# The channel transform of a pair's first token tile, taken relative to the second tile's, in a Fourier mixing layer

## The chip, the cores and the metric

The kernel runs on one core of one Trainium2 chip. The metric is the device time of one execution in microseconds (us), smaller is better. Three runs of the kernel before took 1577.05, 1577.85 and 1578.53 us; the median is 1577.85 us. The core has a matrix engine (PE, whose weight loads are shown apart as PEld), a vector engine (DVE), a scalar engine (ACT), a general engine (POOL) and a queue engine (SP) that issues most loads. Each engine works through its own instructions in the order in which they stand; semaphores make it wait for others.

## The reference

Two sequences, x_prompt of 2048 tokens and x_sample of 512 tokens with 1024 channels each, go through two layers and a final norm. The first layer is windowed attention and is not touched here. The second mixes positions and channels by a Fourier transform and multiplies the result by a gate:

```python
def fourier_layer(x, g, w_gate, w_out):
    b, s, d = x.shape
    h = rmsnorm(x, g)
    hg = h.astype(jnp.float32).reshape(b, s, N_FGROUPS, FGROUP_CH)
    f = jnp.fft.fftn(hg, axes=(1, 3), norm="ortho").real
    f = f.reshape(b, s, d).astype(x.dtype)
    gate = h @ w_gate
    return x + (f * jax.nn.silu(gate)) @ w_out
```

All arithmetic is float32. On PE a float32 operand is cut into a rounded high part and a low rest ("hi" and "lo"), and a product is the sum of two or three matmuls over these parts.

## The kernel before

**Pairs.** The Fourier layer goes over the tokens in 20 tiles of 128 tokens. A Pair is two tiles; there are ten pairs, numbered 0 to 9. Pairs 0 and 1 hold the four tiles of the sample; pairs 2 and 3, 4 and 5, 6 and 7, 8 and 9 hold four tiles each of the prompt, tiles a, a+4, a+8 and a+12. For each pair two things are made from its normed input: the gate product (128 tokens by 1024 channels times 1024 by 1024, for both tiles), and the channel transform z of each tile (each group's 256 channels by a 256x256 matrix of cosines and sines, named chan or ch).

**The gate product in seven products.** The tile's channels are turned so that they lie on partitions. A11 and A12 are the two halves of the first tile's channels, A21 and A22 those of the second's; half 0 of a group is its first 128 channels, half 1 the other 128. The two-by-two block product is computed in the Winograd form with seven products, whose left factors are A11, A12, A22 and four sums, made by Pair.sums (lines 1106 to 1119) and cut into hi and lo by Pair.parts (line 1121):

- F[1] = A21 + A22
- F[2] = F[1] - A11
- F[3] = A11 - A21
- F[4] = A12 - F[2], which is (A11 + A12) - (A21 + A22)

S[i] are the hi and lo of F[i]. F[1] and F[2] share one tile named s1, F[3] and F[4] another named s4; both take a slot of a pool with four slots (tag "x", xtile), which the input tiles and the tile c of gate sums use as well. Line 1103 makes A21 - A22, whose hi and lo are named diff (tile tTd).

**The channel transform.** For the second tile (i = 1), z_odd_even (line 1143) uses that the even outputs of a 256-point transform need only the sum of the two halves, and the odd outputs only their difference: it multiplies S[1] and diff, each by a 128-column half of the matrix. The matrix's hi and lo stand side by side as 256 moving columns, so that one product takes two matmuls (hi and lo of the token side); 16 matmuls of 128x256 fill four PSUM banks. ACT copies the part of the matrix's lo out of a bank (line 1160), DVE adds the part of the hi (line 1161). For the first tile (i = 0), Pair.z (line 1124) multiplies A11 and A12 by the matrix directly, three matmuls for a product: 24 matmuls of 128x256 in two banks, through matmul3 (line 117), each emptied by one ACT instruction (line 1139).

**The four-point step.** When both pairs of a group are done, combine (line 1327) calls radix4 (line 1263): six DVE instructions of 128x1024 over the four z tiles, whose outputs POOL stores (line 1337), for the last group keeps.

**The loop and the queues.** gates(pr, hooks) (line 1184) writes out the seven products of one pair on PE: W = A11 B11, Z = S[1] T1, W += S[2] T2, Z += S[4] B22, W += S[3] T3, W += A22 N4, and X = A12 B21 in four steps (x_step) between them. Between the products stand hooks, in which the next pair nx is made ready: hook 1 and 2 turn its tiles (PE transposes, "trb", line 1089) and make F[1], diff, F[2], F[4] and their parts; hook 3 the parts of F[4], hook 4 F[3] and its parts; hook 5 is z_odd_even, hook 6 is z for the first tile and combine. The input tiles x of the pair after that are loaded by SP into freed slots of the pool "x" and normed (line 1056 on ACT: sum of squares; line 110 DVE and line 111 POOL: inverse root; line 1081 DVE: scaling). DVE adds the gate sums (c12 at line 1227, c22 at 1232, c11 at 1236), ACT takes tanh (line 1197), DVE finishes the gate (line 1198), POOL stores it.

A scheduler sets the final order on each engine from this text and its own estimates, and gives out the pool slots; PSUM for turns and z is a pool of five banks, for W, Z and X another of three. What an operand has to wait for is therefore set by three things: the data, the slot or bank, and what stands ahead in the queue.

In the rows below, "odd pair" and "even pair" name the number of nx, the pair being made ready; combine runs after the odd ones.

Of the kernel before, what the change touches and what calls it, by code (L numbers as in the profile page):

```python
# [14 lines left out]
ALU = mybir.AluOpType  # L15
# [27 lines left out]
def encoder(  # L43
# [61 lines left out]
    def htile(shape, dtype, name):  # L105
        return main.tile(shape, dtype, align_bytes=LINE, tag="hT", bufs=8, name=name)
# [884 lines left out]
    def fourier_phase(tail):  # L991
        with ExitStack() as es:
# [15 lines left out]
            def zt(name):  # L1008
                return right([P, D], F32, name)
# [58 lines left out]
            class Pair:  # L1068
# [71 lines left out]
                        out, ps.rearrange("p (g o n) -> p g o n", g=2, o=2), AF.Copy, scale=1.0 if t >= SEQ // P else 0.5  # L1140
                    )

                def z_odd_even(self):

                    t = self.ts[1]
                    self.zs[1] = zt(f"z{t}")
                    for g in range(4):
                        ps = bank(f"z{t}_{g}")
                        for odd, m in enumerate((self.S[1], self.diff)):

                            to = ps[:, odd * 256 : odd * 256 + 256].rearrange("p (a n) -> p a n", a=2)
                            for part in range(2):
                                PE.matmul(
                                    to, m[part][:, g * P : (g + 1) * P], ch[:, 0, :, odd * P : (odd + 1) * P],
                                    start=part == 0, stop=part == 1,
                                )
                        v = ps.rearrange("p (o a n) -> p a o n", o=2, a=2)
                        out = self.zs[1][:, g * 256 : g * 256 + 256].rearrange("p (n o) -> p o n", o=2)
                        scale = 1.0 if t >= SEQ // P else 0.5
                        ACT.activation(out, v[:, 1], AF.Copy, scale=scale)  # L1160
                        last_z[0] = DVE.scalar_tensor_tensor(out, v[:, 0], scale, out, ALU.mult, ALU.add)
# [98 lines left out]
            def tt(out, a, b, op):  # L1260
                DVE.tensor_tensor(out, a, b, op)

            def radix4(z, name):

                e = zt(f"e{name}")
                tt(e, z[0], z[2], ALU.add)
                tt(z[0], z[0], z[2], ALU.subtract)
                tt(z[2], z[1], z[3], ALU.add)
                tt(z[1], z[1], z[3], ALU.subtract)
                tt(z[3], e, z[2], ALU.subtract)  # L1270
                tt(e, e, z[2], ALU.add)
                return e, z[3], z[0], z[1]
# [50 lines left out]
            def turns4(pr):  # L1323
                pr.sums(3)
                pr.parts(3)

            def combine(pr):

                if pr.n % 2 == 0:
                    return  # L1330
                gi = pr.n // 2
                r = radix4(pairs[pr.n - 1].zs + pr.zs, f"r{gi}")
                if gi == 4:
                    kept.extend(r)
                    return
                for i in range(4):
                    POOL.dma_start(gsd[i] if gi == 0 else evd[gi - 1, i] if i < 2 else odd[gi - 1, i - 2], r[i])
# [20 lines left out]
            for n, pr in enumerate(pairs[:-1]):  # L1358
                nx = pairs[n + 1]
                if n:  # L1360
                    for i in range(2):
                        nx.load(1 - i)
                        nx.norms(1 - i)
                gates(pr, {
                    1: [lambda: turns1(nx)], 2: [lambda: turns2(nx)], 3: [lambda: turns3(nx)], 4: [lambda: turns4(nx)],
                    5: [lambda: nx.z_odd_even()],
                    6: [lambda: nx.z(0), lambda: nx.z(1), lambda: combine(nx)],
                })
            gfb = fp.tile([P, D], F32, tag="gb", bufs=1, name="gfb")
            SP.dma_start(gfb, bass.AP(gf.tensor, gf.offset, [[0, P], [1, D]]))  # L1370
# [616 lines left out]
```

## Time and profile before

| what | value |
|---|---|
| median of three runs | 1577.85 us |
| the profiled execution, its own time | 1577.83 us |
| span inside that execution | 1576.1 us |
| mean granted PE clock | 0.999 |
| the stage of the seven products, about | 1060 to 1320 us of the span |
| busy in that stage, 1060 to 1335 us (275 us) | PE 274.8, DVE 219.9, ACT 151.7, POOL 52.1 us |

The profile is one execution. Its page gives busy time by engine; the view of waits says which engine waited for which; the chain of waits follows the work that ended last, piece by piece; the timeline lists instructions with their start, duration, engine, line, operands and, in brackets, the idle time before them and what ended it. A matmul row shows the time in the pipeline; the time that a stretch of matmuls takes is read from the starts or from the chain. Consecutive instructions of DVE and ACT overlap a little, so the step from start to start is shorter than the duration.

### The profile page before, as it was taken

Reading aid. Unit: us, or ns where it says so; the run is one execution under the profiler, and the core shown is the slowest. Engines: PE = TensorE matmul, PEld = TensorE weight load, DVE = VectorE, ACT = ScalarE, POOL = GpSimd, SP = SyncE. Lnnn points to the kernel's source line nnn. Section 1 sums busy time; section 2 is a strip of 40 time slices with the busy share of each in tenths; the row PEclk is TensorE's granted clock in tenths of the full one; section 3 lists DMA queues with packets and bytes.
Section 4 is the critical chain, followed back from the end, with each engine's and each line's share of the span. In section 5 each row is a group of like instructions: output and inputs, shape, how many; then the busy total and the mean of one; then the engine's idle time right before and its main releaser. Section 6 shows DMA issues by size and latency. Waiting matters only on the chain.

```text
span 1576.1 us, 27737 instructions
## 1 busy us (share of the span) xinstructions
PE 1565.2 (99%) x9882; PEld 1315.6 (83%) x9882; DVE 1150.7 (73%) x2793; ACT 878.1 (56%) x2096; POOL 444.6 (28%) x614
## 2 busy tenths in 40 slices
PE   9999999999999999999999999999999999999998
PEld 7888888888888888988888888888888888888886
DVE  6888555877548786378764577668878778989886
ACT  7788535776247684257852477646655554333353
POOL 2575642421404314024223242222111111101100
PEclk9999999999999999999999999999999999999999
DMA  8598695565856667656649656675666569557852
GB/s 296 203 332 287 223 365 210 208 247 202 297 214 214 204 248 256 242 193 235 238 170 326 232 208 208 248 253 200 210 222 233 185 219 399 193 201 267 312 195 94
DMA packets 100997, 373.90 MB, mean 237 GB/s; under 512 B 11268, under 2 KB 22284, under 8 KB 83453
## 3 DMA queue, kind: packets, MB, share of 16 engines
q1 hardware_dynamic: 83148, 298.17, 53.7%
q0 software_dynamic: 16400, 70.04, 11.5%
q10 hardware_dynamic: 1312, 3.94, 0.6%
q8 instruction: 78, 1.28, 0.3%
q14 instruction: 59, 0.48, 0.1%
HBM read 280.84 MB, written 91.26 MB: 236 GB/s over the span
## 4 chain that ended last, share of the span: by engine, by line
PE 94%; DVE 4%; issue 1%; ACT 1%; DMA 0%; POOL 0%; SPq 0%; POOLq 0%; DVEq 0%; ACTq 0%
PE gp L117 14%; PE qp L117 14%; PE spt L117 11%; PE op L117 7%; PE W L117 7%; PE av L615 6%; PE spt L530 6%; PE fo L117 5%; PE vp L117 3%; PE Z L117 3%; PE pt L589 3%; PE Wo L117 3%; PE z L117 2%; PE X L117 2%; PE Zo L117 2%; PE ABp L117 1%
## 5 line engine op out<-in xcount | busy, mean ns | idle before, releaser
L117 PE MATMUL gp<-h,wg 128*128 128x512 f32 x960 | 237.7, 396 | 0.0
L117 PE MATMUL qp<-h,wq 128*128 128x512 f32 x960 | 237.0, 396 | 0.0
L549 DVE CUSTOM_DVE_ANT_0 S<-spt,b 128x385 f32<-128x385 f32 (+1 forms) x320 | 156.5, 528 | 105.5 <-PE spt L530 68.3
L117 PEld LDWEIGHTS gp<-h,wg 128*128 128x128 f32 x960 | 174.9, 188 | 37.3 <-issue 1.0
L117 PEld LDWEIGHTS qp<-h,wq 128*128 128x128 f32 x960 | 174.9, 188 | 36.4 <-issue 0.3
L557 ACT ACTIVATE S<-S 128x385 f32<-128x385 f32 (+1 forms) x320 | 188.8, 596 | 19.5 <-DVE S L549 19.3
L597 ACT CAST pts<-pt 128x384 fp32r<-128x384 f32 (+1 forms) x240 | 100.6, 458 | 167.0 <-PE pt L589 158.2
L598 DVE TENSOR_TENSOR pts<-pt,pts 128x384 fp32r<-128x384 f32 (+1 forms) x240 | 114.3, 520 | 23.4 <-ACT pts L597 22.2
L639 POOL TENSOR_TENSOR uT<-o,uT 128x256 fp32r<-128x256 f32 x75 | 55.6, 741 | 229.5 <-ACT uT L638 229.4
L117 PE MATMUL spt<-wo,uT 128*128 128x512 f32 x480 | 120.3, 391 | 0.0
L117 PE MATMUL op<-wo,uT 128*128 128x512 f32 x480 | 118.9, 391 | 0.0
L530 PE MATMUL spt<-kwin,qab 64*128 64x384 f32 (+1 forms) x960 | 118.8, 353 | 0.0
L615 PEld LDWEIGHTS av<-pts,v 128*128 128x128 f32 x576 | 101.4, 188 | 18.8
L615 PE MATMUL av<-pts,v 128*128 128x512 f32 (+1 forms) x576 | 115.7, 341 | 0.0
L117 PE MATMUL fo<-wo,tTu 128*128 128x512 f32 x480 | 115.4, 392 | 0.0
L117 PEld LDWEIGHTS op<-wo,uT 128*128 128x128 f32 x480 | 89.4, 188 | 18.5
L117 PEld LDWEIGHTS spt<-wo,uT 128*128 128x128 f32 x480 | 89.1, 188 | 18.3
L117 PEld LDWEIGHTS fo<-wo,tTu 128*128 128x128 f32 x480 | 88.3, 188 | 17.3
L569 DVE TENSOR_SCALAR S<-S 128x384 f32<-128x384 f32 (+1 forms) x192 | 95.9, 499 | 6.8
L530 PEld LDWEIGHTS spt<-kwin,qab 64*128 64x128 f32 x960 | 74.7, 186 | 28.4 <-issue 26.4
L635 POOL TENSOR_TENSOR o<-o,s 128x256 f32<-128x256 f32 x75 | 55.4, 738 | 134.5 <-DVE o L633 134.1
L589 PEld LDWEIGHTS pt<-ident,S 64*128 64x128 f32 x1328 | 78.3, 138 | 4.2 <-issue 2.1
(331 smaller groups left out, 3173.2 us busy)
## 6 DMA issues: line engine op xcount, KB each, us to landing
wo<-wsd SPq DMA_DIRECT2D x32, 1024.0 KB, 5.0
wq<-wsd SPq DMA_DIRECT2D x31, 1024.0 KB, 7.1
wg<-wsd SPq DMA_DIRECT2D x31, 1024.0 KB, 5.8
x<-x1d SPq DMA_DIRECT2D x40, 512.0 KB, 3.9
b<-b21d SPq DMA_DIRECT2D x40, 512.0 KB, 4.8
b<-rowd SPq DMA_DIRECT2D x40, 384.0 KB, 4.3
xs<-in_x_dram SPq DMA_DIRECT2D x23, 512.0 KB, 7.5
s2d<-gt POOLq DMA_DIRECT2D x40, 256.0 KB, 5.2
```

The source lines that it names most:

```text
L117: ins = pe(PE.matmul(out, a[i], b[j], start=start and i + j == 0, stop=stop and i == 1, skip_group_check=more))
L530: pe(PE.matmul(banks[j][:, 2 + k0 * P : 2 + k1 * P], res["q"][rows, qp, b * P : (b + 1) * P], kwin[g][rows, kp, b * P + k0 * P : b * P + k ...
L549: seq(DVE, DVE.tensor_tensor_reduce(out=s[:, e0:e1], in0=ps[:, 1 + e0 : 1 + e1], in1=st["bias"][:, j, 386 - e1 : 386 - e0][:, ::-1], scale ...
L557: last_exp[0] = seq(ACT, ACT.activation(s[:, e0:e1], s[:, e0:e1], AF.Exp, bias=s[:, 386:387], scale=-1.0, accum_out=s[:, 387:388]))
L569: seq(DVE, DVE.tensor_scalar(s[:, ks], s[:, ks], den, None, ALU.mult))
L589: pe(PE.transpose(ps[h][:, kb, j, :], ss[j][rows, 1 + kb * P : 1 + (kb + 1) * P], ident[rows, rows]))
L597: seq(ACT, ACT.copy(hi, ps[:, k0:k1]))
L598: seq(DVE, DVE.tensor_tensor(lo, ps[:, k0:k1], f32(hi), ALU.subtract))
L615: pe(PE.matmul(to, v, pt, start=n == part == 0, stop=part == 1 and n in (1, len(todo) - 1), skip_group_check=n > 1,))
L635: eng.tensor_tensor(o, o, s, ALU.mult)
L639: low = eng.tensor_tensor(lo, o, f32(hi), ALU.subtract)
```

## The change

For pairs 2 to 9 the first tile's transform is replaced by the transform of the first tile minus the second tile. The even outputs of that difference need F[4] (sum of halves of the difference), which is there as S[4]. The odd outputs need (A11 - A12) - (A21 - A22), which is 2 F[3] - F[4]: the new method cross makes it in place of F[4] with one DVE instruction, and cuts it into hi and lo in a new tile named tC (pool "hT", eight slots). z_odd_even is called a second time, with i = 0 and these two operands, in place of the two calls of z. The four-point step gets z0 - z1 and z2 - z3 in place of z0 and z2, and radix4_relative makes the same four outputs from them, in six DVE instructions again. Pairs 0 and 1 stay as they were.

```diff
+                def cross(self):
+
+                    F3, F4 = self.F[3], self.F[4]
+                    DVE.scalar_tensor_tensor(F4, F3, 2.0, F4, ALU.mult, ALU.subtract)
+                    self.mixed = split(htile([P, 2, 512], F32R, f"tC{self.n}"), F4)
+
-                def z_odd_even(self):
+                def z_odd_even(self, i=1):
 
-                    t = self.ts[1]
-                    self.zs[1] = zt(f"z{t}")
+                    t = self.ts[i]
+                    out_of = (self.S[1], self.diff) if i else (self.S[4], self.mixed)
+                    self.zs[i] = zt(f"z{t}")
                     for g in range(4):
                         ps = bank(f"z{t}_{g}")
-                        for odd, m in enumerate((self.S[1], self.diff)):
+                        for odd, m in enumerate(out_of):
...
+            def radix4_relative(z, name):
+
+                e = zt(f"e{name}")
+                tt(e, z[0], z[2], ALU.add)
+                tt(z[0], z[0], z[2], ALU.subtract)
+                tt(z[2], z[1], z[3], ALU.add)
+                tt(z[1], z[1], z[3], ALU.subtract)
+                DVE.scalar_tensor_tensor(z[2], z[2], 2.0, e, ALU.mult, ALU.add)
+                tt(z[0], z[0], z[1], ALU.add)
+                return z[2], e, z[0], z[1]
...
             def turns4(pr):
                 pr.sums(3)
                 pr.parts(3)
+                if pr.n > 1:
+                    pr.cross()
...
-                r = radix4(pairs[pr.n - 1].zs + pr.zs, f"r{gi}")
+                r = (radix4_relative if pr.n > 1 else radix4)(pairs[pr.n - 1].zs + pr.zs, f"r{gi}")
...
-                    6: [lambda: nx.z(0), lambda: nx.z(1), lambda: combine(nx)],
+                    6: [lambda: nx.z_odd_even(0) if nx.n > 1 else [nx.z(hf) for hf in range(2)], lambda: combine(nx)],
```

The lines of the changed kernel are shifted: the matmuls of z_odd_even are at line 1160 there (1153 before), its ACT and DVE instructions at 1167 and 1168 (1160 and 1161 before), tanh and gate at 1204 and 1205 (1197 and 1198), the gate sums c12, c22 and c11 at 1234, 1239 and 1243 (1227, 1232 and 1236); line 1146 is the new DVE instruction of cross. Numbers behind a name are buffer numbers of the program, not of the trace. Three places of the new order follow, all around pair 6, an even one.

PE at the end of gates for pair 5, where N4 (wN) ends and the first tile's transform stands. Names: chan_sb is the transform's matrix, tTb_0 and tTb_1 are A11 and A12 of pair 6, S_6_14299 is S[4], tC the new operand, wB the factor of the next pair's first product. Before:

```order
L117 MATMUL W_14167<-wN_3_12887,tTb_1_13953 128x512 x3
L117 MATMUL z_0_14369<-chan_sb,tTb_0_14241 128x256 x3
L117 MATMUL z_0_14369<-chan_sb,tTb_1_14253 128x256 x3
L117 MATMUL z_0_14369<-chan_sb,tTb_0_14241 128x256 x3
L117 MATMUL z_0_14369<-chan_sb,tTb_1_14253 128x256 x3
L117 MATMUL z_1_14383<-chan_sb,tTb_0_14241 128x256 x3
L117 MATMUL z_1_14383<-chan_sb,tTb_1_14253 128x256 x3
L117 MATMUL z_1_14383<-chan_sb,tTb_0_14241 128x256 x3
L117 MATMUL z_1_14383<-chan_sb,tTb_1_14253 128x256 x3
L117 MATMUL W_14415<-wB_0_12646,tTb_0_14241 128x512 x3
```

The same place now:

```order
L117 MATMUL W_14183<-wN_3_12887,tTb_1_13965 128x512 x3
L1160 MATMUL z_0_14389<-chan_sb,S_6_14299 128x256 x2
L1160 MATMUL z_0_14389<-chan_sb,tC_14330 128x256
L117 MATMUL W_14435<-wB_0_12646,tTb_0_14257 128x512 x3
L117 MATMUL W_14435<-wB_1_12664,tTb_0_14257 128x512
L1160 MATMUL z_0_14389<-chan_sb,tC_14330 128x256
L117 MATMUL W_14435<-wB_1_12664,tTb_0_14257 128x512
L1160 MATMUL z_1_14396<-chan_sb,S_6_14299 128x256 x2
L1160 MATMUL z_1_14396<-chan_sb,tC_14330 128x256 x2
L117 MATMUL W_14435<-wB_1_12664,tTb_0_14257 128x512
L117 MATMUL W_14435<-wB_2_12691,tTb_0_14257 128x512
L1160 MATMUL z_2_14403<-chan_sb,S_6_14299 128x256 x2
```

24 matmuls of 128x256 become 16 (each of z_0 to z_3 takes two with S[4] and two with tC), and in even pairs they are interleaved with the first matmuls of the next pair's W. The third matmul of the block needs the hi part of tC. In odd pairs the 16 stand together.

ACT in the same stretch. S_6 are casts of hi parts of the sums, jkb is the sum of squares of an input tile x, gt the tanh of gate sums, z the emptying of banks. Before:

```order
L1197 ACTIVATE gt_1_14279<-c_5_14234 128x512
L1013 CAST S_6_14310<-s_6_14256 128x512
L1056 ACTIVATE jkb_14400,ssb_14399<-x_14_14397 128x1024
L1197 ACTIVATE gt_1_14304<-c_14170 128x512
L1197 ACTIVATE gt_0_14319<-c_14170 128x512
L1160 ACTIVATE z_14323<-z_0_14324 128x2x128
```

Now:

```order
L1204 ACTIVATE gt_1_14295<-c_5_14250 128x512
L1167 ACTIVATE z_14343<-z_0_14344 128x2x128
L1167 ACTIVATE z_14343<-z_1_14351 128x2x128
L1204 ACTIVATE gt_1_14320<-c_14186 128x512
L1167 ACTIVATE z_14343<-z_2_14358 128x2x128
L1167 ACTIVATE z_14343<-z_3_14365 128x2x128
L1013 CAST S_6_14326<-s_6_14272 128x512
L1056 ACTIVATE jkb_14420,ssb_14419<-x_14_14417 128x1024
L1013 CAST tC_14330<-s_6_14272 128x512
L1204 ACTIVATE gt_0_14339<-c_14186 128x512
```

The cast of tC stands behind the sum of squares of x_14 (a tile that SP loads at that time), and four bank emptyings and a tanh stand ahead of both.

DVE in the same stretch, now, from the low part of S[2] to the first emptied bank (before, L1119, the sum F[3], came ahead of gt and c, and no L1146 and no tC were there):

```order
L1015 TENSOR_TENSOR S_6_14274<-s_6_14231,S_6_14274 128x512
L1234 TENSOR_TENSOR c_5_14250<-c_5_14250,Z_14184 128x512
L1015 TENSOR_TENSOR S_6_14299<-s_6_14272,S_6_14299 128x512
L1239 TENSOR_TENSOR c_14186<-c_14186,W_14183 128x512
L1205 SCALAR_TENSOR_TENSOR gt_1_14295<-gt_1_14295,c_5_14250 128x512
L1119 TENSOR_TENSOR s_6_14272<-trb_0_14252,s_6_14272 128x512
L1205 SCALAR_TENSOR_TENSOR gt_1_14320<-gt_1_14320,c_14186 128x512
L1146 SCALAR_TENSOR_TENSOR s_6_14272<-s_6_14272 128x512
L1015 TENSOR_TENSOR S_6_14326<-s_6_14272,S_6_14326 128x512
L1243 TENSOR_TENSOR c_14186<-c_14186,X_14185 128x512
L1015 TENSOR_TENSOR tC_14330<-s_6_14272,tC_14330 128x512
L1168 SCALAR_TENSOR_TENSOR z_14343<-z_0_14344,z_14343 128x2x128
```

The sum c22 (L1239) moved up by two rows, F[3] moved down behind it, and cross (L1146) stands behind F[3] and both gates; the low part of tC is the last reader of the tile s4, after which its slot can take the second input tile of the pair after.

On SP only the end of the stage differs: the load of one factor of X, b21_38, now stands behind two loads of wo in place of ahead of them.

More of the change, by code (lines that the diff above doesn't have):

```diff
@@ L1157, in z_odd_even @@
                         v = ps.rearrange("p (o a n) -> p a o n", o=2, a=2)
-                        out = self.zs[1][:, g * 256 : g * 256 + 256].rearrange("p (n o) -> p o n", o=2)
+                        out = self.zs[i][:, g * 256 : g * 256 + 256].rearrange("p (n o) -> p o n", o=2)
                         scale = 1.0 if t >= SEQ // P else 0.5
```

## The prediction

> **What bounds the kernel now.** First the busy time by engine on the page, which says PE; then, since such a share is a mean over stages, three views of the stage of the seven products.
>
> ```profile
> span 1576.1 us, 27737 instructions
> ...
> PE 1565.2 (99%) x9882; PEld 1315.6 (83%) x9882; DVE 1150.7 (73%) x2793; ACT 878.1 (56%) x2096; POOL 444.6 (28%) x614
> ```
>
> The view of waits for PE, then PEld, from 1050 to 1310 us (total, times, longest):
>
> ```profile
> PE trb L1089 <- DVE xrl L701: 0.3, 1, 0.3
> ...
> PEld z L1153 <- ACT S L1013: 0.3, 1, 0.3
> ```
>
> PE waits for nothing worth naming, so what leaves its queue leaves the time, if nothing else becomes late. The chain of waits over two pairs (start, us, work) gives the prices:
>
> ```profile
> 1136.48 1.91 PE z L1153 x16
> 1138.40 2.75 PE W L117 x12
> 1141.14 2.87 PE z L117 x24
> ...
> 1162.15 1.91 PE z L1153 x16
> 1164.06 2.75 PE W L117 x12
> 1166.81 2.87 PE z L117 x24
> ...
> 1175.83 0.87 PE trb L1089 x8
> ```
>
> The chain is PE without a gap; a pair lasts 1162.15 - 1136.48 = 25.67 us. The second tile's transform takes 1.91 us, the first tile's 2.87 us: both 0.1195 us a matmul. What stands beside it is the windows view (span, then busy us and instructions of PE, PEld, DVE, ACT, POOL, the granted clock): the first window holds an odd pair with the four-point step, the second an even pair.
>
> ```profile
> 1135.00:1160.00 25.00, 25.00 (x139) 21.67 (x138) 23.04 (x34) 13.86 (x27) 5.56 (x10) 1.00 0.72 246
> 1160.00:1185.00 25.00, 25.00 (x139) 21.67 (x138) 16.03 (x28) 13.50 (x28) 3.36 (x6) 1.00 0.47 168
> ```
>
> DVE is the engine to watch: nearly full in odd pairs, with room in even ones. The clock is granted in full.
>
> **The change part by part.**
>
> *PE.* Eight pairs (2 to 9) go from 24 matmuls to 16 of the same shape as the 16 that took 1.91 us: 8 x (2.87 - 1.91) = 7.7 us less. The Trainium skill, page "TensorE: Matmul & The Clock Gate", section "Back-to-back issue gap", gives an isolated gap of N/2.4 + 2.5 ns, 109 ns at 256 columns, by which this term would be 64 x 0.109 = 7.0 us and the sum below 1572.3 us. The chain's 0.1195 us differs, and the measurement decides.
>
> *DVE and ACT.* The prices of what is added (busy us, mean ns), from the groups by shape, 1000 to 1300 us:
>
> ```profile
> L1015 DVE TENSOR_TENSOR S<-s,S 128x512 fp32r<-128x512 f32 x40 | 27.5, 688 | 0.2
> L1081 DVE SCALAR_TENSOR_TENSOR x<-x,invb,g1b 128x1024 f32<-128x1024 f32 x20 | 25.6, 1280 | 13.2 <-POOL invb L111 13.2
> L1013 ACT CAST S<-s 128x512 fp32r<-128x512 f32 x40 | 24.9, 623 | 32.9 <-DVE s L1119 18.1 <-PE W L117 12.2 <-PE Z L117 2.5
> L1261 DVE TENSOR_TENSOR z<-z,z 128x1024 f32<-128x1024 f32 x13 | 15.9, 1225 | 0.4
> L1161 DVE SCALAR_TENSOR_TENSOR z<-z,z 128x256 f32<-128x256 f32 x40 | 14.4, 415 | 0.0
> L1139 ACT ACTIVATE z<-z 128x512 f32<-128x512 f32 x20 | 12.6, 632 | 8.3 <-PE z L117 8.2
> L1160 ACT ACTIVATE z<-z 128x256 f32<-128x256 f32 x40 | 12.6, 393 | 0.8 <-PE z L1153 0.8
> ...
> L1056 ACT ACTIVATION_READ_ACCUMULATOR jkb<-x 128x1 f32 x20 | 3.7, 186 | 0.0
> ```
>
> Per pair DVE gets cross (not in the trace; bounds 0.64, half of the 1.28 of L1081, and 0.69 of L1198 in the next rows, which has the same shape; I take 0.69), the low part of tC (0.69) and four emptied banks (4 x 0.415 = 1.66): 3.04 us. ACT gets one cast and four bank copies for two: 0.62 + 1.57 - 1.26 = 0.93 us. One of the six instructions of the four-point step becomes a scalar_tensor_tensor: between 1.225 and 1.28 us, at most 0.06 more four times, nothing. Over two pairs DVE's load goes from (23.04 + 16.03) x 25.67/25 = 40.1 us to 46.2 us, and the time for it from 51.3 to 49.4 us. It still fits, at 94%, so the cost is nothing as long as lateness in odd pairs is made up in even ones; with that cover gone it would be up to 3.04 us a pair. So the queue has to be walked through.
>
> *The odd pair.* The waits that DVE has to spare, timeline (start, duration, idle before in brackets):
>
> ```profile
> 1135.84 0.69 DVE L1232 TENSOR_TENSOR c<-c,W 128x512 f32<-128x512 f32 x1 [0.45 <-PE W L117]
> 1138.16 1.29 DVE L1198 SCALAR_TENSOR_TENSOR gt<-gt,c 128x512 f32<-128x512 f32 x2 [0.31 <-ACT gt L1197]
> 1139.37 1.41 DVE L1161 SCALAR_TENSOR_TENSOR z<-z,z 128x256 f32<-128x256 f32 x4
> 1140.70 1.27 DVE L1081 SCALAR_TENSOR_TENSOR x<-x,invb,g1b 128x1024 f32<-128x1024 f32 x1
> 1142.35 0.15 DVE L110 TENSOR_SCALAR invb<-ssb 128x1 f32<-128x1 f32 x1 [0.38 <-ACT jkb L1056]
> 1142.83 0.69 DVE L1198 SCALAR_TENSOR_TENSOR gt<-gt,W 128x512 f32<-128x512 f32 x1 [0.33 <-ACT gt L1197]
> 1152.16 0.68 DVE L1097 TENSOR_TENSOR tTb<-trb,tTb 128x512 fp32r<-128x512 f32 x1
> ```
>
> Back to back, instructions start closer together than they last: four emptied banks take 1140.70 - 1139.37 = 1.33 us, one of 512 columns 0.60 us (next rows). So DVE gets 1.33 + 2 x 0.60 = 2.53 us and has 0.45 + 0.31 + 0.38 + 0.33 = 1.47 us of waits to spend: at 1152.16, where the even pair begins, it is 1.1 us late if all the waits are filled, 2.5 if none. New waits for tanh and for the copies of the new banks come in their place; I take 2.0. PE arrives there 0.96 us earlier besides.
>
> *The even pair.* Its rows before:
>
> ```profile
> 1155.10 0.69 DVE L1097 TENSOR_TENSOR tTd<-trb,tTd 128x512 fp32r<-128x512 f32 x1 [0.28 <-ACT tTd L1096]
> ...
> 1158.10 0.68 DVE L1015 TENSOR_TENSOR S<-s,S 128x512 fp32r<-128x512 f32 x1
> ...
> 1158.86 0.32 SPq L1076 DMA_DIRECT2D x<-x1d  x1
> 1159.30 0.68 DVE L1015 TENSOR_TENSOR S<-s,S 128x512 fp32r<-128x512 f32 x1
> ...
> 1162.88 0.32 SPq L1076 DMA_DIRECT2D x<-x1d  x1
> ...
> 1166.93 1.06 ACT L1056 ACTIVATE jkb<-x 128x1024 bf16<-128x1024 f32 x1 [1.46 <-DMA x<-x1d]
> ...
> 1170.13 0.57 POOL L111 TENSOR_TENSOR invb<-invb,mhalf 128x1 f32<-128x1 f32 x1
> ...
> 1177.36 0.69 DVE L1097 TENSOR_TENSOR tTb<-trb,tTb 128x512 fp32r<-128x512 f32 x1 [5.34 <-ACT tTb L1096]
> ```
>
> With 2.0 - 0.28 = 1.7 us of lateness the low part of S[4] starts at 1161.0 instead of 1159.30. Then by the new order, at 0.60 a step: c22 at 1161.6, done 1162.3; gate, F[3], gate; cross at 1164.0, done 1164.7. N4 needs W's bank after c22: PE comes to it at 1164.06 - 0.96 = 1163.1, so that holds with 0.8 us to spare. PE wants the cast of tC after two matmuls of the new block, at 1166.81 - 0.96 + 0.24 = 1166.1. If ACT were free the cast would be done at 1164.7 + 0.6 = 1165.3, in time. But ahead of it stand four bank copies and a tanh (the banks fill from 1162.15 - 0.96 on, and c22 is done at 1162.3, which puts the last copy at about 1163.9), the cast of S[3] (to 1164.5), and the sum of squares of x (1.06 + 0.19 for its readout, to 1165.8): the cast ends at about 1166.4. PE waits 0.3 us, and 0.8 if DVE is 2.5 late; 0 if 1.1. I take 0.5 in pairs 4, 6 and 8. Pair 2 follows the old four-point step of pair 1, without the added work: nothing. Together 1.5 us, bounds 0 and 2.4. PE has other matmuls between its waits for the banks behind this one. The idle 5.34 us at 1177.36 is what the lateness falls into; the next odd pair starts clean.
>
> *The rest.* b21_38 on SP now stands behind two loads of wo:
>
> ```profile
> 1299.43 1.00 SPq L1713 DMA_DIRECT2D wo<-fbd  x2
> ...
> 1312.29 0.86 PE L117 MATMUL X<-b,tTb 128*128 128x512 f32 x3
> ...
> b<-b21d SPq DMA_DIRECT2D x20, 512.0 KB, 5.4
> ```
>
> Issued at about 1300.5 with 5.4 us to landing it is there at 1306, used at 1312: nothing.
>
> **Sum**, against the profiled execution's 1577.83 us (1.7 us of it lie around the span; the median shown is 1577.85, the same): 1577.83 - 7.7 + 1.5 = **1571.6 us**, that is -0.39%. About 0.2% (3.2 us) is what a measurement of this kernel tells from no change.
>
> **The rivals.**
>
> *No stall.* The cast of tC is in time everywhere: 1577.83 - 7.7 = 1570.1 us. For it: the bound of 1.1 us; against it: the sum of squares ahead of the cast, and that new waits tend to come where old ones are filled.
>
> *The load ahead of the cast is late.* The sum of squares needs an x tile whose load starts when the low part of S[2] is done: 1158.86 before, about 1160.6 now. How long the loads of x take, in 1130 to 1190 us:
>
> ```profile
> DMA to landing us min/median/max: 3.3/3.6/4.0
> ```
>
> At 3.3 to 3.6 us it lands by 1164.2, when ACT comes to it. At the 5.4 us of b21's loads, which have the same size, it lands at 1166.0 and the cast ends at 1167.9: PE waits 1.8 us, three times, 5.4 us in all, which leaves 1575.5 us. For it: lateness on DVE moves loads to where others run; against it: 4.0 was the longest of these loads.
>
> *The second x load makes the transposes late, and it is slower.* Its slot was that of s4, freed by the low part of S[3] (load at 1162.88); now it is freed by the low part of tC, about 1167.1 in even pairs. At 4.0 us it lands at 1171.1; sum of squares to 1172.4, inverse root to 1173.1 (0.15 on DVE, 0.57 on POOL), and since that small instruction stands ahead of both scalings on DVE, the first scaled tile is there at 1174.4; PE transposes it at 1175.83 - 0.96 + 0.5 = 1175.4. There is 1 us to spare, so up to a landing of 5 us nothing happens. From there each us is lost at the transposes and again where c22 and N4 follow late, about 2 us in each of four even pairs; the gain of 6.2 us is gone at 5.8 us. At 6 us: 1571.6 + 8 = 1579.6 us. For it: the slot is freed 4 us later than before, beside other traffic; against it: the same longest 4.0.
>
> *That the change doesn't do what it says* can be left out for the count: the order shows 16 for 24.
>
> **How the numbers follow.** Forecast (stall of 0.1 to 0.8 us in three pairs, 1570.4 to 1573) 0.52; no stall 0.17; late load or a like lateness at c22 or a bank (1573 to 1578) 0.23, a good third of it under 1574.7; slower 0.08. Faster by over 0.2% (under 1574.7): 0.52 + 0.17 + 0.08 = 0.77; within 0.2%: 0.15; slower: 0.08. The range leaves out half a us below the case without a stall, for the run's own spread, and the upper part of the late load: 1569.5 to 1576.5. The likeliest case alone has 1570.4 to 1573.
>
> **What would show it.** In the chain of waits the first tile's transform at 1.91 us in odd pairs, and pairs of about 24.7 us (odd) and 25.2 us (even); PE's instructions down by 64; in PE's or PEld's waits a new row, z at L1160 from ACT's cast (L1013), of about 0.3 to 0.8 us, three times; DVE near 46 us busy in two pairs; the second x load issued right after the low part of tC. Wrong would be: PE waiting for c22 (L1239), for trb from x (L1081), or for z banks from L1168, or a first-tile transform above 2 us without any wait.

## Result and profile after

| | before | changed | ratio (95% interval) |
|---|---|---|---|
| first series, median (runs) | 1578.19 us (14) | 1573.99 us (14) | 0.9974 (0.9966 to 0.9982) |
| second series, median (runs) | 1578.15 us (16) | 1575.42 us (11) | 0.9978 (0.9969 to 0.9987) |
| profiled execution | 1577.83 us | 1575.53 us | |
| its span | 1576.1 us | 1573.5 us | |

The change saves 4.2 us in the first series and 2.7 in the second; the forecast was 6.2. Both medians are faster by more than 0.2% and lie in the range given; the likeliest case alone (1570.4 to 1573) holds neither.

The busy times of the changed kernel, from the head of its page:

```profile
span 1573.5 us, 27706 instructions
...
PE 1561.3 (99%) x9818; PEld 1308.6 (83%) x9818; DVE 1169.3 (74%) x2841; ACT 884.9 (56%) x2120; POOL 446.3 (28%) x614
```

PE has 64 matmuls and 3.9 us less; PE is still the bound. The chain of waits of the changed kernel in the stage of the seven products (start, us, work), first the end of pair 2, then an odd and an even pair:

```profile
1116.75 0.61 PE z L1160 x3
1117.36 0.46 PE W L117 x2
1117.82 0.32 PE z L1160
...
1137.27 1.91 PE z L1160 x16
1139.18 2.75 PE W L117 x12
1141.92 1.91 PE z L1160 x16
...
1161.97 1.91 PE z L1160 x16
1163.88 2.75 PE W L117 x12
1166.63 0.35 PE z L1160 x3
1166.98 0.93 PE W L117 x4
```

The second 1.91 in the odd pair is the first tile's transform, 2.87 before. The pair lasts 1161.97 - 1137.27 = 24.70 us. In the even pair the three matmuls at 1166.63 take 0.35 us, which is their price without a wait; in pair 2 the same three take 0.61, and one more takes 0.32 where its price is 0.12.

Waits of PE, then of PEld, in the changed kernel, 1050 to 1310 us (total, times, longest):

```profile
PE trb L1089 <- DVE x L1081: 0.6, 1, 0.6
...
PEld trb L1089 <- PE Z L117: 1.0, 1, 1.0
...
PEld z L1160 <- DVE tC L1015: 0.4, 1, 0.4
...
PEld z L1160 <- ACT tC L1013: 0.2, 1, 0.2
```

The first two rows are one stall of 1.0 us, at the transposes of pair 7; the last two are the 0.56 us that the weight loads of pair 2 wait (PE's own two pieces above are 0.46 us longer than their price). No other pair waits for tC in this profile. Then something the forecast had not looked at, behind the stage: PEld's waits from 1315 to 1345 us. There the sample's position transform stands (As and Bs, made from the parts gs; us are its results times the gate) and the product with the output weights (fo, with the weights wo cut into hi and lo from the loaded blocks w32f).

```profile
PEld Bs L117 <- DVE us L1468: 1.0, 1, 1.0
PEld fo L117 <- ACT wo L1743: 0.6, 1, 0.6
```

Neither row is there before. Cutting each profile at three marks shows where the time went. "Stage" runs from the first transform of a second tile to the first matmul that makes As, "next part" from there to the first matmul of tw (the first turns for the prompt's position transform), "rest" from there to the end of the span. The kernels of the experiments below are in the same table.

| profile | stage | next part | rest | span |
|---|---|---|---|---|
| before | 242.87 | 53.40 | 212.5 | 1576.1 |
| before, again | 242.71 | 53.43 | 213.2 | 1576.3 |
| changed | 236.80 | 54.53 | 213.7 | 1573.5 |
| changed, again | 236.89 | 55.15 | 213.4 | 1572.8 |
| changed, third | 237.68 | 54.49 | 213.8 | 1573.3 |
| no_cross | 235.37 | 54.16 | 214.6 | 1571.7 |
| two_cross | 238.13 | 53.92 | 213.2 | 1573.4 |
| sq_and_store | 235.62 | 54.76 | 213.2 | 1570.4 |
| casts_later | 238.20 | 55.40 | 212.8 | 1574.8 |
| w32f_first | 238.08 | 53.68 | 214.0 | 1573.0 |
| all_four | 237.12 | 52.91 | 214.8 | 1571.5 |
| low_first | 236.84 | 54.63 | 212.4 | 1570.1 |
| low_and_loads | 235.74 | 52.93 | 215.1 | 1570.6 |
| x_on_pool | 245.03 | 54.74 | 213.6 | 1580.1 |

Mean of three profiles of the changed kernel against mean of two of before: the stage gains 242.79 - 237.12 = 5.7 us, the next part loses 54.72 - 53.42 = 1.3, the rest loses 0.8 (a mean of 213.6 against 212.9), about what the two profiles of before differ by (0.7). That makes 3.6 us in all, between the two measured 4.2 and 2.7. The spans themselves differ by 2.9, because the profiles of the changed kernel come 0.7 us later into the stage, with the same code ahead of it.

### The profile page after: what moved, and what is told of

It reads as the page before. It is cut to its first block, busy times and chain, and to the rows that moved or that the text cites. A ratio compares the mean times of both kernels' runs of the same rounds, so it can differ in the third digit from the quotient of the medians.

```text
span 1573.5 us, 27706 instructions
## 1 busy us (share of the span) xinstructions
PE 1561.3 (99%) x9818; PEld 1308.6 (83%) x9818; DVE 1169.3 (74%) x2841; ACT 884.9 (56%) x2120; POOL 446.3 (28%) x614
## 4 chain that ended last, share of the span: by engine, by line
PE 89%; DMA 4%; DVE 3%; issue 2%; ACT 1%; POOL 0%; POOLq 0%; ACTq 0%; SPq 0%; DVEq 0%
PE gp L117 14%; PE qp L117 14%; PE spt L117 11%; PE op L117 7%; PE av L615 6%; PE spt L530 6%; PE W L117 5%; PE vp L117 3%; PE fo L117 3%; PE pt L589 3%; PE Wo L117 3%; PE Z L117 3%; PE z L1160 2%; PE Zo L117 2%; PE X L117 1%
```

## Experiments

**Both kernels again.** No edit.

> The changed kernel a second time, to see which differences repeat. The stage of the seven products (from the first transform of a second tile to the first matmul that makes As) took 236.80 us in the first profile, 242.87 before the change. Theory (the gain is cut by two small waits of PE inside the stage, 0.56 us in pair 2 and 1.0 us at the transposes of pair 7, and by 1.4 us lost behind it, between 1305 and 1345 us, where the DMA engines are full in both kernels and the loads don't come earlier): the same two waits, 236.8 us within 0.3, and again about 1.4 us less of a lead at the end of that stretch. Rival (executions differ by so much anyway): the 1.0 us at pair 7 or the loss behind the stage is not there this time.

> The kernel before a second time. Theory: stage of 242.9 us within 0.3, no wait of PE for a cast of w32f behind it, and the same length as in its first profile from the end of the stage to the end of the program (266.0 us from As to the end of the span, within 0.5). Rival (executions differ by so much anyway): this last stretch differs by 1 to 2 us between its two profiles, which is as much as what the changed kernel lost there.

Measured: 1574.88 us for the changed kernel, 1578.19 for before, one execution each. The 1.0 us at pair 7 is there again, as are the wait of pair 2 for the low part of tC (0.4 us; the 0.2 for its cast is not) and the two waits behind the stage (0.9 and 1.3 us), and the next part is 1.7 us longer than before. In the kernel before it is 53.40 and 53.43 us. So these are the change's own. The 1.2 us by which the first profile of the changed kernel came late into the stage are not: that start lies between 1066.89 and 1068.43 us in the five profiles, with the same code ahead of it, and the two kernels overlap. From As to the end of the span the kernel before took 266.7 us, 0.7 more than in its first profile, where the expectation allowed 0.5; all of that lies in the rest, so a difference of 0.7 us there says nothing.

**Without the cross sum.**

```
-                    DVE.scalar_tensor_tensor(F4, F3, 2.0, F4, ALU.mult, ALU.subtract)
-                    self.mixed = split(htile([P, 2, 512], F32R, f"tC{self.n}"), F4)
+                    self.mixed = self.S[3]
```

> The changed kernel without the sum 2F3-F4 and the two parts made from it: the first tile's even outputs are made from the parts of S3 instead, so that part of the result is left out. DVE has two instructions of 0.6 us less in a pair, ACT one; PE has the same 16 matmuls. Theory: the waits in pair 2 and at pair 7 go (both come from DVE and ACT being late), the stage takes 235.2 us, and the loss behind the stage stays, since it comes from the loads: the whole is 1.5 us faster than the changed kernel. Rival (the added work on DVE and ACT eats the gain everywhere, also behind the stage through a backlog): the loss behind the stage goes too, 3 us faster in all.

Measured: 1573.8 us, 1.1 less than the changed kernel beside it. The stage takes 235.37 us, 7.5 less than before, against 7.7 that the matmuls are worth: with the cross sum and its parts gone, both waits are gone, and from pair 2 on the pairs take 24.70 or 24.71 us each. So the stage's whole shortfall comes from the added work (and from the slot of s4, which is freed later by it) and not from PE. The next part still loses 0.7 us against before: fo waits 0.9 us for a cast. Bs no longer waits, but not because DVE had a backlog before. DVE's row at the low part of block 4, ahead of us, in the changed kernel and then in this one:

```profile
1324.44 1.29 DVE L1744 TENSOR_TENSOR wo<-w32f,wo 128x512 fp32r<-128x512 f32 x2 [1.47 <-ACT wo L1743]
```

```profile
1320.86 1.29 DVE L1742 TENSOR_TENSOR wo<-w32f,wo 128x512 fp32r<-128x512 f32 x2 [0.22 <-ACT wo L1741]
```

In the changed kernel DVE stands idle there for 1.47 us, waiting for ACT's cast, which waits for the load; here the load comes 3.6 us earlier, while the part itself starts 2.3 us earlier. Why the load gains more is not shown.

**The cross sum doubled.**

```
                     DVE.scalar_tensor_tensor(F4, F3, 2.0, F4, ALU.mult, ALU.subtract)
+                    DVE.scalar_tensor_tensor(F4, F3, 0.0, F4, ALU.mult, ALU.add)
```

> The changed kernel with one more instruction of the size of the cross sum on DVE in each of eight pairs, right behind it (F4 plus 0 times F3): 0.6 us more in the queue ahead of the cast of tC. Theory (DVE makes up in even pairs for what odd pairs leave): only the cast of tC in the even pairs is late by up to 0.6 us, 0.3 to 0.6 us of waiting in each of the four even pairs, so 1 to 2.4 us slower. Rival (DVE is the bound in the stage by now): 0.6 us in each of eight pairs, 4.8 us slower.

Measured: 1575.51 us, 0.6 more than the changed kernel beside it, where the theory had 1 to 2.4. The stage takes 238.13 us: 1.3 more than in the first two profiles of the changed kernel and 0.5 more than in the third. PEld's waits in the stage:

```profile
PEld z L1161 <- ACT tC L1013: 2.3, 4, 0.7
```

Four waits, one for each even pair, of at most 0.7 us, as the first theory had it; besides, PE waits 1.1 us instead of 0.6 at the transposes of pair 7. Far from 4.8 us: DVE isn't the bound in the stage, it makes up in even pairs. This is the stall that the prediction had put at 0.5 us in pairs 4, 6 and 8. It does not need the added work on DVE: in the third profile of the changed kernel it stands in pair 8, which is 0.5 us longer there. PEld's two waits for the cast of tC in that stage (0.3 us in pair 2, 0.5 in pair 8), and ACT's row ahead of the cast in pair 8:

```profile
PEld z L1160 <- ACT tC L1013: 0.8, 2, 0.5
```

```profile
1264.56 1.06 ACT L1056 ACTIVATE jkb<-x 128x1024 bf16<-128x1024 f32 x1 [0.49 <-DMA x<-x1d]
```

The sum of squares waits for its x tile, which took 4.3 us to landing, and the cast of tC stands behind it. In pair 6 the same happens in two of the runs below whose stage has the same code, casts_later (a load of 4.2 us, a wait of 0.7) and w32f_first (4.1 and 0.3). This is the prediction's rival of the late load ahead of the cast, in single pairs.

**Two edits of order in the stage.** `last_cast[0]` is ACT's cast of the latest tC:

```
-                    inv = sumsq(xt, f"b{self.ts[i]}")
+                    inv = sumsq(xt, f"b{self.ts[i]}", lambda key, ins: (after(ins, last_cast[0]) if key == "act" else 0, ins)[1])
...
-                    POOL.dma_start(dst[t0 * P : (t0 + 1) * P, half * 512 : half * 512 + 512], th)
+                    queue = SP if (i, half) == (1, 0) else POOL
+                    queue.dma_start(dst[t0 * P : (t0 + 1) * P, half * 512 : half * 512 + 512], th)
```

> The changed kernel with two edits of order in the stage: the sum of squares of an x tile stands behind the cast of tC on ACT (not ahead of it, as in the even pairs), and the gate that is stored last in a pair (left half of the second tile) is stored from SP's queue instead of POOL's, where it stood ahead of the inverse roots. Theory: the 1.0 us at the transposes of pair 7 comes from POOL's inverse roots standing behind that store, which POOL issued late there (1222.33 us, 2.5 us after DVE was done), and goes; of the 0.56 us in pair 2 the wait for the cast (about 0.2) goes, and the wait for the low part (0.3 to 0.4, DVE has no gap there) stays. Stage of 235.4 to 235.7 us instead of 236.80; nothing changes in the loss behind the stage. Rival (the transposes of pair 7 wait because the second x tile is loaded late, whatever POOL does): the 1.0 us stays, and since the sums of squares are put back by 0.6 us, grows by that: 237.2 us.

Measured: 1572.21 us, the stage 235.62 us. The timeline at pair 7 (start, duration, idle before in brackets): the last gate on DVE, then POOL, in the changed kernel; behind them POOL in this one and, last, the same store before the change:

```profile
1218.76 0.67 DVE L1205 SCALAR_TENSOR_TENSOR gt<-gt,W 128x512 f32<-128x512 f32 x1
...
1222.33 0.55 POOL L1208 DMA_DIRECT2D s2d<-gt  x1 [3.65 <-DVE invb L110]
1222.90 1.08 POOL L111 TENSOR_TENSOR invb<-invb,mhalf 128x1 f32<-128x1 f32 x2
```

```profile
1216.22 0.54 POOL L1213 DMA_DIRECT2D s2d<-gt  x1 [3.12 <-DVE gt L1209]
1218.91 0.56 POOL L111 TENSOR_TENSOR invb<-invb,mhalf 128x1 f32<-128x1 f32 x1 [2.15 <-DVE invb L110]
1219.68 1.51 POOL L111 TENSOR_TENSOR invb<-invb,mhalf 128x1 f32<-128x1 f32 x1 [0.22 <-DVE invb L110]
```

```profile
1223.74 0.55 POOL L1201 DMA_DIRECT2D s2d<-gt  x1 [5.18 <-issue]
```

In the changed kernel the gate that the store at 1222.33 writes was done at 1219.4, and both inverse roots stood behind that store on POOL. With the store on SP they run as soon as DVE hands them over, and from the transposes of pair 6 to those of pair 7 pass 24.70 us, 25.67 in the changed kernel: the rival falls. What held the store for 2.9 us isn't shown; before the change it was late at the same place, and there the inverse roots had time to spare. In pair 2 the expectation missed: the wait for the cast of tC (0.2) turned into one for its low part (0.7 on PEld), so putting the cast first alone gains nothing there.

**The casts of block 4 later.**

```
-            f_split(4)
             new += position(*early[1])
+            f_split(4)
             f_split(5)
```

> The changed kernel with the casts of the fifth block of the output weights (w32f, block 4) put behind the second position of the last part, on ACT and DVE. Theory (the loss behind the stage is two waits made by loads that come late in a stretch where the DMA engines are full): the wait of Bs for us goes, 0.5 to 1.0 us, since DVE no longer stands at the low part of that block ahead of us; the wait of fo for the casts of blocks 6 and 7 stays at 0.6 to 1.3 us. Lead lost between 1305 and 1345 us: 0.5 to 1.2 us instead of 1.4 and 2.05. Rival (DVE comes to this part with a backlog from the stage): Bs waits as before.

Measured: 1576.76 us, a miss. Bs does not wait any more, so its wait did come from DVE standing at that block's low part; but fo now waits, 1.1 us for the casts and 0.7 for the low parts, and the next part is 55.40 us. The stage, whose code is the same, is also 1.3 to 1.4 us longer than in the first two profiles of the changed kernel, in pairs 2 and 6. Blocks 6 and 7 are used soon after, and everything that is put behind their loads comes late with them.

**The loads of blocks 6 and 7 first.** The load of x for the residual and the ev loads get an order dependency on the last of them:

```
-                SP.dma_start(w32f[k].rearrange("p k c -> p (k c)"), w_fout[k // 4, k % 4])
+                last_w32f[0] = SP.dma_start(w32f[k].rearrange("p k c -> p (k c)"), w_fout[k // 4, k % 4])
...
-                SP.dma_start(x2, rows(x1d, r))
+                after(SP.dma_start(x2, rows(x1d, r)), last_w32f[0])
...
-                    SP.dma_start(t, evd[a, i])
+                    after(SP.dma_start(t, evd[a, i]), last_w32f[0])
```

> The changed kernel with the loads of blocks 6 and 7 of the output weights issued ahead of the two loads of x for the residual and of the ev tiles, on SP: about 4 us earlier. Theory (late loads): the wait of fo for the casts of blocks 6 and 7 goes (0.6 us in the first profile, 1.3 in the second), the wait of Bs (1.0) stays, since it hangs on block 4: 0.6 to 1.3 us faster than the changed kernel's 1574.9 us on this chip, unless the x loads, 4 us later now, make the residual late. Rival (the casts are late because ACT is): fo waits as before.

Measured: 1574.73 us, where the sum had 1573.6 to 1574.3: the next part is 53.68 us, 1 us better, and the wait of fo is gone, as the theory of late loads has it; Bs waits 0.9 us still. The 1 us was lost again in the stage, whose code is the same, at the transposes of pair 3 (below). The late load itself, in ACT's timeline of the changed kernel and of the kernel before:

```profile
1323.79 1.14 ACT L1743 CAST wo<-w32f 128x512 fp32r<-128x512 f32 x2 [1.71 <-DMA w32f<-in_w_fout_dram]
```

```profile
1326.86 1.14 ACT L1723 CAST wo<-w32f 128x512 fp32r<-128x512 f32 x2
```

And the DMA engines in that stretch of the changed kernel (windows view; the last two numbers are their busy share and GB/s):

```profile
1305.00:1310.00 5.00, 5.00 (x35) 4.57 (x34) 2.78 (x6) 1.40 (x5) 1.09 (x2) 1.00 1.03 418
1310.00:1315.00 5.00, 4.90 (x26) 3.83 (x26) 4.73 (x8) 0.99 (x2) 0.51 (x1) 1.00 1.04 410
1315.00:1320.00 5.00, 5.00 (x30) 4.17 (x29) 5.00 (x9) 4.76 (x10) 1.14 (x3) 1.00 1.04 420
```

The engines are full. ACT comes to the cast 4.8 us earlier than before the change (1323.79 - 1.71 = 1322.08 against 1326.86), the block only 3.1 us earlier or less. The difference is the wait.

**All four edits.**

> The four edits of order together (sum of squares behind the cast of tC, last store of a pair on SP, casts of block 4 later, loads of blocks 6 and 7 first). Theory: the whole of the 7.7 us arrives but for 0.3 us in pair 2: 1574.9 - 1.3 (stage) - 1.4 to 2.0 (behind it) = 1571.6 to 1572.2 us. Rival (the full DMA stretch only moves the wait to another load): 1573 us or more, with a new wait of PE before 1350 us.

Measured: 1573.32 us. The figure is the rival's, the place is not: there is no new wait between the stage and 1350 us, and the next part is down to 52.91 us, better than before the change. But the stage is 237.12 us: PE waited 1.5 us at the transposes of pair 3, for the second x tile. ACT's and PE's rows there:

```profile
1122.00 1.06 ACT L1056 ACTIVATE jkb<-x 128x1024 bf16<-128x1024 f32 x1 [3.32 <-DMA x<-x1d]
```

```profile
1124.70 1.06 PE L1089 MATMUL trb<-ident,x 128*128 128x128 f32 x8 [1.46 <-DVE x L1081]
```

That load was issued at 1115.7 us, so 6.3 us passed until ACT could start on it. The same load took 4.5, 4.9 and 5.5 us in the three profiles of the changed kernel (PE lost nothing, nothing and 0.9 us there, by the length of the pair), 4.8 in sq_and_store (nothing), 5.5 in casts_later (1.1), 5.7 in w32f_first (1.4). Before the change it took 4.9 and 4.4, and PE came to the transposes 9.1 us after its issue; in the changed kernel 7.3 us after it, of which 2.8 go into the sum of squares, the inverse root and the scaling. So up to 4.5 us nothing is late, and from about 5 PE waits.

**The low part first, and the loads.** The low part of tC ahead of the sum for c11 on DVE, by an order dependency on `last_cast[1]`, the low part of the latest tC, on top of sq_and_store; then the same with the loads of blocks 6 and 7 first; with the changed kernel beside them.

```
-                DVE.tensor_tensor(c11, c11, X, ALU.add)
+                after(DVE.tensor_tensor(c11, c11, X, ALU.add), last_cast[1])
...
+                        after(last_z[0], last_cast[1])
```

> The changed kernel once more, timed beside the two that follow. 3.5 to 4.5 us faster than before.

> The changed kernel with the sum of squares behind the cast of tC, the last store of a pair on SP, and the low part of tC ahead of the sum for c11 on DVE (0.6 us earlier, in the even and the odd pairs). Theory (of the stage's waits, pair 7's came from the store on POOL; pair 2's comes from the low part of tC; and the wait at the transposes of pair 3, from nothing up to 1.5 us in six executions, comes from the second x load, which that low part lets go and which lands 4.5 to 6.3 us later): pair 2's 0.56 us falls to 0.2 or less, pair 3's is 0.5 us less, pair 7's 1.0 is gone: 1.5 to 2.2 us faster than the changed kernel beside it. Rival (the low part only trades places, and c11 and the banks come late in its stead): a new wait of 0.3 us or more for X's bank or the z banks in each pair, 0 to 1 us slower than the kernel with the first two edits alone.

> The same with the loads of blocks 6 and 7 ahead of the residual's x and the ev tiles on SP. Theory (late loads in the full stretch): the wait of fo for the casts goes (0.6 to 1.3 us), that of Bs for us stays (1.0): 0.5 to 1.2 us faster than the kernel without it. Rival (the full DMA stretch only moves the wait to another load): no faster, with a wait of that size between 1340 and 1450 us.

Measured: 1575.42 (ratio to before 0.9978, 0.9969 to 0.9987), 1572.28 (0.9964, 0.9951 to 0.9976) and 1573.10 us (0.9967, 0.9955 to 0.9980). The changed kernel is 2.7 us faster than before, less than the 3.5 to 4.5 expected. So low_first has the lowest median: 5.9 us faster than before and 3.1 faster than the changed kernel beside it, more than the 1.5 to 2.2 expected, though those two intervals overlap (eight of the changed kernel's eleven runs lie above the slowest of low_first's six). From the one execution of sq_and_store (1572.21) it can't be told apart. Pair 2's wait is gone in both. In low_first's profile the x load took 6.2 us and PE lost 1.2 us to it; in low_and_loads it took 5.0 and PE lost nothing to it. The loads bring 1.7 us in the next part (52.93 against 54.63), where Bs doesn't wait either, against the expectation, and nothing in the end: the rest is 215.1 us against 212.4. PEld's waits for gp (the operand of the prompt's position transform, ABp) from 1420 to 1570 us, low_first and then low_and_loads:

```profile
PEld ABp L117 <- DVE gp L1429: 2.2, 5, 0.6
```

```profile
PEld ABp L117 <- DVE gp L1429: 3.3, 8, 0.9
PEld ABp L117 <- ACT gp L1428: 1.3, 2, 0.9
```

Together that is 2.4 us more, where the rest grew by 2.7. The rival was right in the outcome, if not in the place: in these two profiles the gain was taken back late in the program, by waits for DVE and ACT and not by another load. That the edit of the loads causes this is not shown: the rest is 214.6 us in no_cross as well, which moves no load, and low_first's 212.4 is the shortest of all.

**The second x load on POOL.**

```
-                        nx.load(1 - i)
+                        nx.load(1 - i, POOL if i else SP)
```

> The kernel with the three edits of order in the stage (sum of squares behind the cast of tC, last store of a pair on SP, low part of tC ahead of c11's sum), and the second x load of each pair issued from POOL instead of SP, where it stood ahead of the four loads of b21 and held them back until its slot was free. Theory (that load lands late, 4.5 to 6.3 us after its issue at the end of pair 2, because the four loads of b21 set out right behind it): the b21 loads leave earlier, in a stretch where the DMA engines are half idle, the second x load lands 3.3 to 4 us after its issue, and the transposes of pair 3 wait for nothing: 0.5 to 1.3 us faster than the 1572.28 us with the three edits. Rival (its landing takes as long whatever runs beside it, or POOL issues it late, as it did with the store in pair 7): transposes wait as before or longer in pair 3 or 7, 1572.3 us or more.

Measured: 1582.07 us, ratio to before 1.0021 (1.0011 to 1.0030), slower than before: the theory falls. The load took 5.2 us at the end of pair 2 though two of the four b21 loads had left 5 us ahead of it, and over the stage the second loads, on POOL's queue, took longer than the first ones, on SP's. The DMA view of this kernel, 1060 to 1320 us (KB each, median us to landing):

```profile
x<-x1d SPq DMA_DIRECT2D x8, 512.0 KB, 3.7
x<-x1d POOLq DMA_DIRECT2D x8, 512.0 KB, 5.3
```

In low_first, where SP issues both, the second loads took a median of 3.5 us (seven landings on record). What runs beside them differs too, so the queue alone isn't shown to be the cause. Most of the 9.8 us by which this is above 1572.28 us lies in the stage (245.03 against 236.84 us) and comes from another wait, that of ACT's tanh, and through it of PE (waits of ACT, then of PE):

```profile
ACT gt L1208 <- DMA s2d<-gt: 11.5, 4, 3.4
```

```profile
PE Z L117 <- DVE gt L1209: 5.1, 4, 2.7
PE trb L1089 <- DVE x L1081: 1.9, 4, 0.5
```

The gates have three buffers, and the fourth gate of a pair needs the one of the first, whose store lands late now (a median of 7.3 us for the stores between 1155 and 1180 us, 3.4 in low_first); PE's next product then waits for the bank that this gate empties. Why the x load varies between 4.4 and 6.3 us stays open.

## Why the prediction came out as it did

- **PE's 7.7 us: right.** The transform takes 1.91 us, and the stage without the cross sum gained 7.5. By the isolated gap of 109 ns that the Trainium skill gives (page "TensorE: Matmul & The Clock Gate", section "Back-to-back issue gap") the term would be an estimated 7.0 us; the trace, with 1.91 us for 16 matmuls, does not agree with it.
- **DVE and ACT have room: right.** DVE is busy 45 us in two pairs (46 forecast):

```profile
1135.90:1160.60 24.70, 24.70 (x134) 21.25 (x133) 23.52 (x37) 13.47 (x29) 5.56 (x10) 1.00 0.64 233
1160.60:1185.30 24.70, 24.70 (x134) 21.22 (x133) 21.46 (x39) 16.12 (x32) 4.22 (x6) 1.00 0.54 194
```

- **1.5 us of waiting for tC in pairs 4, 6 and 8: the step was wrong, and the size came out near for the stage as a whole by luck.** The stage's gain falls short of 7.7 us by 1.7, 1.8 and 2.6 in the three profiles, but by other waits: pair 2, the transposes of pair 7, and in the third profile those of pair 3. Pairs 4, 6 and 8 wait for tC in neither of the first two profiles, and in the third in pair 8 alone, for a late load. In pair 4 of the first profile the cast was to end 0.55 us behind the start of PE's block (1166.4 against 1166.81 - 0.96); it ended 0.13 us ahead of it (1166.50 against 1166.63). ACT's rows show why:

```profile
1164.31 0.62 ACT L1013 CAST S<-s 128x512 fp32r<-128x512 f32 x1
1164.82 1.08 ACT L1056 ACTIVATE jkb<-x 128x1024 bf16<-128x1024 f32 x1
1165.78 0.21 ACT L1056 ACTIVATION_READ_ACCUMULATOR jkb<-x 128x1 f32 x1
1165.87 0.63 ACT L1013 CAST tC<-s 128x512 fp32r<-128x512 f32 x1
```

From the cast of S to that of tC pass 1.56 us, where the working charged 0.62 + 1.06 + 0.19 = 1.87. DVE's instructions were charged by the spacing of their starts, ACT's by their durations, which overlap as well. The Trainium skill (page "ScalarE: Activation LUTs", section "What ACT_TABLE_LOAD costs") gives 93 ns of overlap between ACTIVATEs that follow each other; the rows are near it, with 0.11 and 0.12 us: 0.62 and 0.21 of duration against 0.51 and 0.09 of spacing. That is 0.31 of the 0.68 us. The rest lies ahead of the cast of S, which started 2.34 us behind the pair's first matmul (1161.97) where the working had 2.69; there, too, ACT's copies and tanh stand back to back.
- **Pair 2, "nothing": wrong, 0.56 us.** It was argued that pair 1 has the old four-point step. But that stretch was nearly full already. The windows view of before, then of the changed kernel (the same times; the work stands 1.2 us later in the second):

```profile
1100.00:1120.00 20.00, 20.00 (x112) 17.45 (x111) 18.57 (x30) 11.20 (x22) 4.39 (x8) 1.00 0.75 252
```

```profile
1100.00:1120.00 20.00, 20.00 (x110) 16.94 (x109) 19.92 (x31) 12.70 (x25) 4.40 (x8) 1.00 0.66 233
```

DVE has 1.4 us to spare before, and pair 2 adds its own cross sum and tC to it. A row of the pair in question would have shown this; the working took the rows of pair 4 for all.
- **The two late loads, held to be unlikely.** Against both the prediction set that 4.0 us was the longest landing. But that row covers 1130 to 1190 us alone, and only two of its loads have a landing on record. The second x load at the end of pair 2, ahead of that window, took 4.9 us in the same profile (issued at 1115.21); ACT's row at its end:

```profile
1120.07 1.06 ACT L1056 ACTIVATE jkb<-x 128x1024 bf16<-128x1024 f32 x1 [2.48 <-DMA x<-x1d]
```

The mechanism of the second x load is real: it costs from nothing to 1.5 us at the transposes of pair 3, depending on the landing, and the 1.0 us of pair 7 comes from the same smaller margin, by POOL's late store and not by the load. The 1 us to spare, up to a landing of 5 us, was right. The price of 2 us in each of four even pairs was too high: one or two pairs are hit. The load ahead of the cast costs 0.5 us in one pair of one of the three profiles, where the prediction had 1.8 us in three.
- **The sum's last step, that all behind the stage moves with it: wrong by 1.3 us.** The prediction had no term for it. It looked at one load behind the stage (b21_38, rightly nothing, though the last loads of b21 took 9.2 to 10.1 us to landing and not the 5.4 charged) and not at the loads of w32f: in a stretch where the DMA engines are full, they come earlier by less than PE does.

So the forecast was right in direction and, by luck, near in the stage (5.7 us gained where it had 6.2); what it lost lies mostly behind the stage.

## What to carry to other kernels

Ask of a gain in one stage what it meets in the next: here the DMA engines were full behind the stage (a busy share of 1.03 and 1.04), ACT came to a loaded block 4.8 us earlier and the block 3.1 us earlier at most, so part of the lead was spent waiting. Take the spread of a load's landing from all rounds, not from the window around one. Check the margin of every pair or round that differs from the one whose rows are shown, the first one above all. And charge each engine by the spacing of its starts, not by the durations of its instructions.

## Unexpected in the hardware

- The small inverse root on POOL is late not for its own 0.6 us but for a store ahead of it in the same queue, which sat 2.9 us after its data were done, at the same pair in both kernels.
- The second x loads, 512 KB each, took a median of 5.3 us to landing from POOL's queue (x_on_pool) and 3.5 from SP's (low_first), with other traffic beside them.
- The landing of one and the same load varies by 1.5 us between executions of kernels with the same code in the stage: 4.8 us in sq_and_store, 6.3 in all_four.
